# A hybrid decoder layer on one core: attention's value product, the embedding pairs and the norms' splits are moved

## The chip, the cores and the metric

One core of one Trainium2 chip runs the whole layer. The time is device microseconds (us) of one execution, as the median of three runs; a profiled execution of the same program gives the trace. The engines are TensorE (PE, with its weight loads as PEld), VectorE (DVE), ScalarE (ACT), GpSimd (POOL) and SyncE (SP), which issues most DMAs.

## The reference

One layer on 512 tokens of width 2048, in float32:

```python
h = rmsnorm(x, attn_norm_g)
u, v_sgu, q, k, v_att, g_a, g_b = split(h @ w_in)      # 2048 -> 9216
y_a = gelu(u) * (tril(w_s) @ rmsnorm(gelu(v_sgu)) + b_s)   # chunks of 128, 8 groups
z = q @ k.T * scale                                    # q, k normed; 8 heads of 128
log_1m = where(strict, log_sigmoid(-z), 0)
tail = reverse_cumsum(log_1m) - log_1m
w = where(strict, exp(log_sigmoid(z) + tail), 0)
y_b = w @ v_att
x = x + (sigmoid(g_a) * (y_a @ w_up_a) + sigmoid(g_b) * (y_b @ w_up_b)) @ w_o
gate, up = split(rmsnorm(x, ffn_norm_g) @ w_ffn_in)    # hidden 5632
x = x + (silu(gate) * up) @ w_ffn_out
x = x + sigmoid(rmsnorm(x, ple_norm_g) @ w_ple_gate) * (p @ w_ple)   # p: 256 wide
```

## The kernel before

Activations lie transposed: a block is 256 features by 512 tokens, kept as 128 partitions by 1024. Every float32 operand is split into a rounded high half and a low half (`split_into`, `Weights`): ACT writes the high half, DVE the difference, and three products make one. A **form** is a block of an operand in this shape. A *plain* use of a unit takes the four blocks of the form, twelve matmuls of 512 columns; a form of kind "S" has three further sums of blocks, and an "S" use takes seven products of half the size with them, on DVE's and ACT's account. `HALF` and the like say for each unit in how many of the first output blocks it is used plainly, since its sums are not there yet. A **pair** is one output block of 256 features: all units of the operand against its weights, accumulated in PSUM banks (six of tag "ps", two of tag "small"). A pair of "S" uses alone is *doubled*: two products stand side by side in a bank, and `mix_doubled` adds them up while the products go on; a pair with both kinds is put together by `rest`.

The order of work is written out in program order. Each unit of a pair calls `tick` once or twice; a tick loads or splits a part of the next forms (`builds`), loads the further sums' raw block (`seconds`, `fetch_second`), and runs what is due in `waiting`. `after(n, f)` runs f n ticks later. `Staged` and `beside` spread a chain of steps over ticks. Weights come through `planned` and `prepared` in a fixed order.

The stages: one embedding product (`ple_pair`: four blocks of `w_ple` against p, twelve matmuls of 512), then the projection `w_in` in four rounds of q, k, v and gate pairs, with the attention of two heads of the round before running beside them; SGU pairs; then the **merge**, plain pairs of `w_up_b` and `w_up_a` (eight of each); the **output projection** `w_o`, eight pairs, which adds onto x, stores x1 and sums its squares (`Norm.add`); the FFN's 44 pairs of `w_ffn_in` (the forms `fs` made from x1); three passes of `w_ffn_out`; and the eight gate pairs (forms `gs` from x2). Embedding products 3 to 7 stand at the end of the output projection. A norm's row is not needed for its products: it scales their outputs. `Norm.steps` sums with ones on PE, takes a power on POOL, and spreads the result with four small matmuls.

In attention a head has four blocks of keys j = 3, 2, 1, 0, each of (4 - j) x 128 queries. `stage_a` makes the logits, `stage_m` masks, `stage_b` and `stage_c` split the sums (L1122 on ACT, L1126 on DVE, into `zh` and `zl`), `stage_d` multiplies with a triangle (L1132, L1133), subtracts (L1137) and takes the exponential (L1138); `finish` multiplies a head's weights with the values (L1145) and copies the result (L1147). One block takes three ticks. Lines used below: L357 and L354, high and low half of weights; L373, weight sums; L284, L285, halves of forms; L520, the scaling by a norm's gain; L525, sums of blocks of forms; L683, products of S uses; L294 to L296, of plain ones; L739 and L742, mixing; L787, `rest`; L792, the addition onto x; L873, eviction of an embedding product; L516, loads.

## Time and profile before

| | |
|---|---|
| runs (us) | 2669.71, 2667.64, 2671.62; median 2669.71 |
| profiled execution (us) | 2668.2; span 2666.5, granted clock 0.998 |
| PE busy | 2640.4 us, 99% of the span |
| DVE, ACT, POOL busy | 84%, 53%, 17% |
| DMA | 560.16 MB, mean 210 GB/s |

Lnnn is a line of the kernel. In a list of waits a row reads: who waited, for whom, us in total, times, the longest. In a timeline: start, duration, engine, line, operation, names, and in brackets the idle time before it and what ended it. In a table by windows: the stretch, its length, busy us (instructions) of PE, PEld, DVE, ACT and POOL, the granted clock, the DMA share and GB/s. A row of groups ends with busy us, mean ns of one, and the engine's idle time before them.

### The profile page before, as it was taken

The numbers are of one execution on the slowest core, as the hardware profiler recorded it, in microseconds if no ns is written. First come the engines' busy times: TensorE is split into PE (matmuls) and PEld (weight loads), VectorE is DVE, ScalarE is ACT, GpSimd is POOL, SyncE is SP. The second block draws the span as 40 slices with busy tenths as digits, with TensorE's granted clock in tenths as the row PEclk, the third lists the DMA queues.
The fourth block names the chain that finished last, engine by engine and source line by source line (L and its number), as shares of the span: only waits on it lengthen the run. The fifth ranks groups of instructions, "written<-read, shape, count | busy, mean of one in ns | idle before, by whom it ended". The sixth has DMA issues, their size and how long they took to land.

```text
span 2666.5 us, 42598 instructions
## 1 busy us (share of the span) xinstructions
PE 2640.4 (99%) x15354; PEld 2312.4 (87%) x15354; DVE 2236.4 (84%) x3791; ACT 1413.9 (53%) x2245; POOL 453.4 (17%) x557
## 2 busy tenths in 40 slices
PE   8999999999999999999999999999999999999999
PEld 7888898888998888888888888888888888889898
DVE  8687878787887658989889888888889989989876
ACT  7656565655554334576444444444445445455643
POOL 0222322222220001101111111111110211211010
PEclk9999999999999999999999999999999999999999
DMA  7577777677775669988888878888787989988884
GB/s 227 158 190 174 185 173 187 171 182 197 179 188 186 214 212 264 239 265 223 220 218 207 210 194 207 203 203 202 197 209 223 263 220 277 226 248 246 252 229 134
DMA packets 293875, 560.16 MB, mean 210 GB/s; under 512 B 26400, under 2 KB 140832, under 8 KB 293664
## 3 DMA queue, kind: packets, MB, share of 16 engines
q1 hardware_dynamic: 231408, 442.08, 50.4%
q0 software_dynamic: 62256, 115.37, 27.0%
q8 instruction: 120, 1.97, 0.3%
q14 instruction: 91, 0.75, 0.1%
HBM read 505.97 MB, written 51.38 MB: 209 GB/s over the span
## 4 chain that ended last, share of the span: by engine, by line
PE 88%; DVE 5%; ACT 2%; DMA 2%; issue 1%; POOL 0%; SPq 0%; POOLq 0%; DVEq 0%; ACTq 0%
PE ps L683 49%; PE ps L295 10%; PE ps L296 10%; PE ps L294 10%; PE small L683 6%; DVE wlo L354 2%; DVE out L742 1%; PE small L1145 1%; PE small L1021 1%; DMA wholes<-x 1%; DMA wholes<-w_in 1%; ACT whi L357 1%; DVE wholes L373 0%; PE small L1095 0%; DVE parts L285 0%
## 5 line engine op out<-in xcount | busy, mean ns | idle before, releaser
L683 PE MATMUL ps<-parts,whi 128*128 128x512 f32 x4200 | 1404.7, 398 | 3.7 <-DVE out L787 3.1
L357 ACT ACTIVATE whi<-wholes 128x512 fp32r<-128x512 f32 (+3 forms) x941 | 872.5, 940 | 727.6 <-DVE wholes L373 270.5
L354 DVE TENSOR_TENSOR wlo<-wholes,whi 128x512 fp32r<-128x512 f32 (+3 forms) x941 | 982.7, 1079 | 65.8 <-ACT whi L357 64.0
L683 PEld LDWEIGHTS ps<-parts,wlo 128*128 128x128 f32 x4200 | 788.9, 188 | 178.4 <-DVE wlo L354 1.1
L683 PE MATMUL ps<-parts,wlo 128*128 128x256 f32 x4200 | 832.0, 279 | 0.0
L683 PEld LDWEIGHTS ps<-parts,whi 128*128 128x128 f32 x4200 | 676.4, 189 | 10.2 <-issue 4.5
L294 PE MATMUL ps<-parts,whi 128*128 128x256 f32 (+1 forms) x1822 | 598.9, 330 | 8.0 <-ACT parts L284 5.6
L295 PE MATMUL ps<-parts,whi 128*128 128x256 f32 (+1 forms) x1838 | 605.9, 330 | 0.8 <-DVE parts L285 0.8
L296 PE MATMUL ps<-parts,wlo 128*128 128x256 f32 (+1 forms) x1838 | 605.8, 330 | 0.0
L295 PEld LDWEIGHTS ps<-parts,whi 128*128 128x128 f32 x1838 | 348.4, 190 | 39.0 <-DVE parts L285 2.4
L294 PEld LDWEIGHTS ps<-parts,whi 128*128 128x128 f32 x1822 | 344.6, 190 | 41.5 <-ACT parts L284 6.7
L296 PEld LDWEIGHTS ps<-parts,wlo 128*128 128x128 f32 x1838 | 348.8, 190 | 30.8
L373 DVE TENSOR_TENSOR wholes<-wholes 128x256 f32<-128x256 f32 x822 | 345.1, 420 | 21.7 <-DMA wholes<-w_ffn_in 2.6
L742 DVE TENSOR_TENSOR out<-out,ps 128x256 f32<-128x256 f32 x490 | 202.9, 416 | 149.9 <-ACT out L739 149.4
L361 POOL DMA_DIRECT2D wholes<-w_ffn_in x170 | 148.0, 870 | 691.2 <-DVE wholes L373 197.4
L361 POOL DMA_DIRECT2D wholes<-w_in x132 | 116.3, 882 | 523.1 <-DMA wholes<-w_in 146.8
L683 PE MATMUL small<-parts,whi 128*128 128x512 f32 x480 | 190.3, 396 | 0.0
L285 DVE TENSOR_TENSOR parts<-wholes,parts 128x1024 fp32r<-128x1024 f32 (+3 forms) x148 | 138.1, 945 | 23.0 <-ACT parts L284 23.0
L284 ACT ACTIVATE parts<-wholes 128x1024 fp32r<-128x1024 f32 (+3 forms) x148 | 119.3, 830 | 55.1 <-DVE wholes L525 33.3
L739 ACT ACTIVATE out<-ps 128x256 f32<-128x256 f32 x258 | 95.7, 382 | 49.9 <-PE ps L683 46.4
L361 POOL DMA_DIRECT2D wholes<-w_ffn_out x64 | 55.6, 869 | 358.3 <-DMA wholes<-w_ffn_out 136.5
L1395 ACT ACTIVATE out<-out 128x512 f32<-128x512 f32 x44 | 27.9, 634 | 159.2 <-DVE out L1394 159.2
(123 smaller groups left out, 1750.2 us busy)
## 6 DMA issues: line engine op xcount, KB each, us to landing
wholes<-w_ffn_in SPq DMA_DIRECT2D x170, 384.0 KB, 5.6
wholes<-w_in SPq DMA_DIRECT2D x132, 384.0 KB, 5.0
wholes<-w_ffn_in SPq DMA_DIRECT2D x170, 256.0 KB, 4.8
wholes<-w_ffn_in POOLq DMA_DIRECT2D x170, 256.0 KB, 5.4
wholes<-w_in SPq DMA_DIRECT2D x132, 256.0 KB, 4.0
wholes<-w_in POOLq DMA_DIRECT2D x132, 256.0 KB, 5.0
wholes<-w_ffn_out SPq DMA_DIRECT2D x64, 384.0 KB, 6.3
wholes<-x SPq DMA_DIRECT2D x45, 512.0 KB, 5.6
```

The source lines that it names most:

```text
L284: return (nc.scalar.activation(hi, src, AF.Copy), nc.vector.tensor_tensor(out=lo, in0=src, in1=hi.bitcast(F32), op=ALU.subtract))
L285: nc.vector.tensor_tensor(out=lo, in0=src, in1=hi.bitcast(F32), op=ALU.subtract))
L294: nc.tensor.matmul(ps, sh, mh, start=start, stop=False)
L295: nc.tensor.matmul(ps, sh, ml, start=False, stop=False)
L296: return nc.tensor.matmul(ps, sl, mh, start=False, stop=stop)
L354: in_turn(nc.vector.tensor_tensor(out=self.lo[:, blocks], in0=r, in1=h.bitcast(F32), op=ALU.subtract))
L357: in_turn(nc.scalar.activation(h, r, AF.Copy))
L361: nc.gpsimd.dma_start(out=raw[:, 3:5], in_=self.src[:, 1:3], accum_op=ALU.add)
L373: in_turn(nc.vector.tensor_tensor(out=o, in0=x, in1=y, op=ALU.add))
L683: m = nc.tensor.matmul(out, l, r, start=first and k == 0, stop=last and k == 1)
L739: in_turn(nc.scalar.activation(out, x, AF.Copy, scale=scale))
L742: in_turn(nc.vector.tensor_tensor(out=out, in0=x, in1=y, op=op))
```

## The change

- Attention: `finish(0)` moves from the middle of the first block of head 1 to the start of its second, two ticks later; the last block of the round gets one tick more between `stage_c` and `stage_d`. So that head 1 does not overwrite what head 0 still needs, the weights of the third key block have two places (`w2`), and only 128 of a row are kept in `first`; the row additions in `stage_d` are cut to match.
- `tick`: a second load may go out in a tick that also runs a step, and is held back by every form of its stage that is not loaded yet, not only by the first three.
- The embedding products 3 to 7 stand behind five of the merge's pairs; their operand is made after the first.
- Forms with a gain are split with it: ACT scales while it writes the high half, DVE's fused operation writes the low half, and the scaling pass before goes.
- `FFN_UNTIL` replaces `HALF` for the FFN: units 2 and 3 are plain in its second pair too.
- The first hidden block and the first gate block take their norm's row three ticks after their pair; the gate's rows e and x2 are loaded three ticks into a pair; the norm keeps its accumulator for the row.

The diff:

```diff
@@ -38,2 +38,4 @@
 PLACE = 7 * 256
+LATER = 3
+FFN_UNTIL = 1, 1, 2, 2, 2, 2, 2, 2
 
@@ -220,6 +222,6 @@
             builds.popleft().step()
-        elif seconds and fits([(wholes, 5 * 256, "old")]):
+        if seconds:
             f = (urgent or seconds)[0]
-            if f.used or not any(b.stage == f.stage and b.ready() and not b.there
-                                 for b in list(builds)[:AHEAD]):
+            if (f.used or not any(b.stage == f.stage and b.ready() and not b.there
+                                  for b in builds)) and fits([(wholes, 5 * 256, "old")]):
                 f.fetch_second()
@@ -533,3 +535,12 @@
         x = form.operand()
-        split_into(x[:, 0:4, 0], x[:, 0:4, 1], cut(raw.f()))
+        if gain:
+            gi, k = gain
+            for i in range(2):
+                hi, lo = (x[:, 2 * i : 2 * i + 2, s] for s in range(2))
+                r, g = cut(raw.f(i * T, (i + 1) * T)), gcol[:, gi + 2 * k + i : gi + 2 * k + i + 1]
+                nc.scalar.activation(hi, r, AF.Copy, scale=g)
+                nc.vector.scalar_tensor_tensor(out=lo, in0=r, scalar=g, in1=hi.bitcast(F32),
+                                               op0=ALU.mult, op1=ALU.subtract)
+        else:
+            split_into(x[:, 0:4, 0], x[:, 0:4, 1], cut(raw.f()))
         give(raw)
@@ -594,4 +605,2 @@
             w = form.raw()
-            if gain:
-                gained(w.f(), w.f(), *gain)
             yield
@@ -959,3 +968,2 @@
                                  start=True, stop=True)
-            give(self.acc)
             yield
@@ -970,3 +978,3 @@
             yield
-            self.block = take(T)
+            self.block = self.acc
             nc.scalar.activation(self.block.f(), ps, AF.Copy)
@@ -1004,4 +1012,4 @@
 
-        for tag, n in (("l", T), ("w0", T), ("w1", 3 * P), ("w2", 2 * P), ("w3", 2 * P),
-                       ("first", 5 * P), ("k", 1024), ("v", 1024), ("zs", 1024)):
+        for tag, n in (("l", T), ("w0", T), ("w1", 3 * P), ("w2", 4 * P), ("w3", 2 * P),
+                       ("first", 2 * P), ("k", 1024), ("v", 1024), ("zs", 1024)):
             att[tag] = take(n)
@@ -1083,3 +1091,3 @@
         def weights(h, j):
-            return a_tile(f"w{j}", (NT - j) * P, (j == NT - 1) * h * P)
+            return a_tile(f"w{j}", (NT - j) * P, (j >= NT - 2) * h * (NT - j) * P)
 
@@ -1087,3 +1095,3 @@
 
-            return (sums(j) if j == NT - 1 else a_tile("first", (NT - j) * P, (j == 1) * 2 * P))[0:1]
+            return (sums(j) if j == NT - 1 else a_tile("first", P, (j == 1) * P))[0:1]
 
@@ -1114,3 +1122,3 @@
                 if j:
-                    nc.gpsimd.tensor_copy(first(j), s[0:1])
+                    nc.gpsimd.tensor_copy(first(j), s[0:1, :P])
                 nc.gpsimd.memset(s[0:1, :P], 0.0)
@@ -1134,4 +1142,6 @@
             if j:
-                nc.vector.tensor_tensor(out=sums(j - 1)[0:1, P:], in0=tp[0:1], in1=first(j),
-                                        op=ALU.add)
+                row = sums(j - 1)[0:1]
+                tt(row[:, P : 2 * P], tp[0:1, :P], first(j), ALU.add)
+                if n > P:
+                    tt(row[:, 2 * P :], tp[0:1, P:], sums(j)[0:1, P:], ALU.add)
             nc.vector.tensor_tensor(out=w, in0=w, in1=tp, op=ALU.subtract)
@@ -1160,6 +1170,6 @@
             ahead = blocks[i + 1 : i + 3]
+            if i == NT + 1:
+                finish(0)
             stage_b(j)
             yield 1
-            if i == NT:
-                finish(0)
             stage_c(j)
@@ -1168,2 +1178,4 @@
             yield 1
+            if not ahead:
+                yield 1
             stage_d(h, j)
@@ -1265,8 +1277,8 @@
                 plan((w_up_a if b == "a" else w_up_b)[j], "PPPP")
+            if 0 < j < 6:
+                planned.append((w_ple[j + 2].rearrange("p (b c) -> p b c", b=4), 1, "P"))
         for j in range(KU):
             plan(w_o[j], now("S" * KU, HALF, j))
-        for j in range(3, KU):
-            planned.append((w_ple[j].rearrange("p (b c) -> p b c", b=4), 1, "P"))
         for m in range(KH):
-            plan(w_ffn_in[m], now("S" * KU, HALF, m))
+            plan(w_ffn_in[m], now("S" * KU, FFN_UNTIL, m))
         at = 0
@@ -1356,2 +1368,8 @@
                 after(1, lambda j=j, s=s: store("mix", j, s))
+        if not j:
+            ple_operands()
+        elif j < 6:
+            ple_pair(j + 2)
+            if j == 5:
+                ple_done()
     give(norm1.block)
@@ -1361,8 +1379,4 @@
     fs = [spilled_form("S", "x1", j, (g_ffn, j)) for j in range(KU)]
-    raw = deque([load(xT[0])])
     for j in range(KU):
-        if j < KU - 1:
-            raw.append(load(xT[j + 1]))
-        if j == KU - 1:
-            after(3, ple_operands)
+        h = load(xT[j])
         if j == 1:
@@ -1370,6 +1384,2 @@
         pr = pair(ms, last=j == KU - 1, j=j, until=HALF, doubled=7)
-        if j == KU - 1:
-            ple_pair(3)
-            ple_pair(4)
-        h = raw.popleft()
         pr.onto(h.f())
@@ -1379,5 +1389,2 @@
         give(h)
-    for j in range(5, 8):
-        ple_pair(j)
-    ple_done()
 
@@ -1392,3 +1399,3 @@
     def hidden(m, o):
-        g = o[:, :T]
+        g, row2 = o[:, :T], norm2.row()
         nc.vector.tensor_tensor(out=g, in0=g, in1=row2, op=ALU.mult)
@@ -1404,7 +1411,8 @@
             build(hs[0])
-        o = pair(fs, last=m == KH - 1, j=m, until=HALF, doubled=7).out()
-        if m == 0:
-            row2 = norm2.row()
+        o = pair(fs, last=m == KH - 1, j=m, until=FFN_UNTIL, doubled=7).out()
         st = Staged(hidden(m, o))
-        st.step()
+        if m:
+            st.step()
+        else:
+            after(LATER, st.step)
         if m == KH - 1:
@@ -1427,3 +1435,3 @@
             o = pr.out()
-            scaled(o, row2)
+            scaled(o, norm2.row())
             if not end:
@@ -1440,6 +1448,9 @@
     for j in range(KU):
-        e, x2 = load(ple_spill[j]), load(spill["x2", j])
+        rows = []
+
+        def rest(j=j, rows=rows):
+            rows.extend((load(ple_spill[j]), load(spill["x2", j])))
 
-        def finish(o, a, b, ps=None):
-            s = o[:, a:b]
+        def finish(o, a, b, ps=None, j=j, rows=rows):
+            s, row3 = o[:, a:b], norm3.row()
             if ps is not None:
@@ -1456,6 +1467,12 @@
             nc.scalar.activation(s, s, AF.Sigmoid)
-            nc.vector.tensor_tensor(out=s, in0=s, in1=e.f(a, b), op=ALU.mult)
-            nc.vector.tensor_tensor(out=s, in0=s, in1=x2.f(a, b), op=ALU.add)
+            for r, op in zip(rows, (ALU.mult, ALU.add)):
+                nc.vector.tensor_tensor(out=s, in0=s, in1=r.f(a, b), op=op)
             nc.sync.dma_start(out=outT[j][:, a:b], in_=s)
 
+        def close(o, finish=finish, rows=rows):
+            finish(o, 0, 2 * T)
+            give(*rows)
+
+        if j:
+            after(LATER, rest)
         if j == KU - 1:
@@ -1464,5 +1481,7 @@
             o = pair(gs, j=j, until=GATE_UNTIL).out()
-            row3 = norm3.row()
-            finish(o, 0, 2 * T)
-            give(e, x2)
+            if j:
+                close(o)
+            else:
+                rest()
+                after(LATER, lambda close=close, o=o: close(o))
     finish_waiting()
```

ACT in round 1 of attention, around the exponential of head 0's last block (L1138, the row with 128x512) and the copy of the product with the values (L1147); L739 belongs to a projection's mixing. Before:

```order
L357 ACTIVATE whi_80<-wholes 128x1280
L1138 ACTIVATE wholes<-wholes 128x512
L739 ACTIVATE out_2867<-ps_2691 128x256
L739 ACTIVATE out_2867<-ps_2696 128x256
L1147 ACTIVATE wholes<-small_2849 128x512
L739 ACTIVATE out_2867<-ps_2701 128x256
```

After, where the two are L1148 and L1157, and L1105 to L1108 are a later block's `stage_a`:

```order
L1108 ACTIVATE wholes<-wholes 128x256
L1148 ACTIVATE wholes<-wholes 128x512
L1130 ACTIVATE parts<-wholes 128x128
L748 ACTIVATE out_2867<-ps_2696 128x256
...
L1106 ACTIVATE wholes<-small_2907,rr_2189 128x384
L1148 ACTIVATE wholes<-wholes 128x128
L1130 ACTIVATE parts<-wholes 128x256
L1157 ACTIVATE wholes<-small_2933 128x512
L359 ACTIVATE whi_78<-wholes 128x512
```

The copy stands three rows below the exponential before, fourteen below it after, behind the first exponential of head 1 (128x128).

SP at the end of the output projection, where the last block of x1 (x_782, then x_786) is stored and loaded again; L875 stores an embedding product, the other loads of x are first or second loads of forms. Before:

```order
L875 DMA ple_10810<-out_10793 128x1024
L1376 DMA x_782_8254<-wholes 128x1024
L339 DMA wholes<-w_ffn_in 128x2x256
L341 DMA wholes<-w_ffn_in 128x768
L875 DMA ple_10843<-out_10826 128x1024
L875 DMA ple_10875<-out_10858 128x1024
L516 DMA wholes<-x_782_8254 128x1024
L339 DMA wholes<-w_ffn_in 128x2x256
L341 DMA wholes<-w_ffn_in 128x768
L875 DMA ple_10908<-out_10891 128x1024
L516 DMA wholes<-x_775_8247 128x1024
```

After:

```order
L339 DMA wholes<-w_ffn_in 128x1024 x2
L518 DMA wholes<-x_782_8266 128x1024
L1386 DMA x_786_8270<-wholes 128x1024
L518 DMA wholes<-x_779_8263 128x1024
L339 DMA wholes<-w_ffn_in 128x1024
L518 DMA wholes<-x_786_8270 128x1024
L518 DMA wholes<-x_780_8264 128x1024
L341 DMA wholes<-w_ffn_in 128x2x256
L343 DMA wholes<-w_ffn_in 128x768
L518 DMA wholes<-x_781_8265 128x1024
```

The embedding stores are gone from there, and a second load (x_779) now stands between the store and the load of the last block.

DVE at the end of the output projection's second pair, where `rest` (L787, then L796) frees two banks; L285 and L287 are low halves of forms, L354 and L356 of weights. Before:

```order
L525 TENSOR_TENSOR wholes<-wholes 128x256
L285 TENSOR_TENSOR parts<-wholes,parts 128x256
L354 TENSOR_TENSOR wlo_77<-wholes,whi_76 128x1280
L354 TENSOR_TENSOR wlo_77<-wholes,whi_76 128x512
L285 TENSOR_TENSOR parts<-wholes,parts 128x3x256
L787 TENSOR_TENSOR out_9527<-ps_9512,out_9527 128x512
L787 TENSOR_TENSOR out_9527<-ps_9505,out_9527 128x512
L373 TENSOR_TENSOR wholes<-wholes 128x256
L792 TENSOR_TENSOR wholes<-wholes,out_9527 128x1024
```

After:

```order
L287 TENSOR_TENSOR parts<-wholes,parts 128x3x256
L375 TENSOR_TENSOR wholes<-wholes 128x256
L287 TENSOR_TENSOR parts<-wholes,parts 128x256
L375 TENSOR_TENSOR wholes<-wholes 128x256
L287 TENSOR_TENSOR parts<-wholes,parts 128x256
L796 TENSOR_TENSOR out_9665<-ps_9648,out_9665 128x512
L356 TENSOR_TENSOR wlo_79<-wholes,whi_78 128x1280
L356 TENSOR_TENSOR wlo_79<-wholes,whi_78 128x512
L796 TENSOR_TENSOR out_9665<-ps_9641,out_9665 128x512
L375 TENSOR_TENSOR wholes<-wholes 128x256
```

The two releases stood side by side behind a weight split and a form's split; now the first stands behind the smaller splits, and a weight split stands between the two.

## The prediction

> **What bounds the kernel now.** I read the page first, then TensorE's waits, then the timeline around each wait that the change can reach, and last the DMA landings where the embedding pairs stood.
>
> ```profile
> span 2666.5 us, 42598 instructions
> PE 2640.4 (99%) x15354; PEld 2312.4 (87%) x15354; DVE 2236.4 (84%) x3791; ACT 1413.9 (53%) x2245; POOL 453.4 (17%) x557
> PE ps L294 <- ACT parts L284: 5.6, 3, 5.1
> PE ps L683 <- DVE out L787: 3.1, 1, 3.1
> PE small L1145 <- ACT wholes L1138: 2.5, 3, 0.8
> PE small L1133 <- DVE parts L1126: 1.6, 4, 0.7
> PE small L1145 <- issue: 0.8, 1, 0.8
> PE ps L294 <- ACT out L873: 0.6, 1, 0.6
> PE ps L295 <- DVE parts L285: 0.8, 2, 0.5
> ```
>
> The page puts TensorE (PE) at 2640.4 of 2666.5 us, so it is the bound, and the change removes none of its work. All that can be won is wait, and the remaining rows (us in total, times, longest) name the waits: 5.1 us of the first is the start of the program. The share of 99% flatters a little, because a record of PE ends after the next one has started:
>
> ```profile
> 1173.75 0.39 PE L296 MATMUL ps<-parts,wlo 128*128 128x512 f32 x1
> 1173.97 0.39 PE L294 MATMUL ps<-parts,whi 128*128 128x512 f32 x1
> 1175.42 0.50 PE L294 MATMUL ps<-parts,whi 128*128 128x512 f32 x1 [0.61 <-ACT out L873]
> 1199.74 0.28 PE L294 MATMUL ps<-parts,whi 128*128 128x256 f32 x1
> 1199.86 0.28 PE L295 MATMUL ps<-parts,whi 128*128 128x256 f32 x1
> ```
>
> Matmuls of 512 columns start about 0.227 us apart (1173.97 minus 1173.75, read over longer stretches) and last 0.39; those of 256 columns start 0.12 apart. So 0.16 us of each wait is hidden in the record before it, and I add 0.16 to every wait of the list. An embedding pair, twelve matmuls of 512, is 2.7 us of PE, and a plain unit of a projection the same.
>
> **Attention's first product with the values (L1145).** In round 1, PE and ScalarE (ACT):
>
> ```profile
> 287.51 0.62 PE L683 MATMUL ps<-parts,whi 128*128 128x512 f32 x2
> 288.98 1.10 PE L1145 MATMUL small<-wholes 128*128 128x512 f32 x2 [0.84 <-ACT wholes L1138]
> 287.06 1.26 ACT L357 ACTIVATE whi<-wholes 128x1280 fp32r<-128x1280 f32 x1
> 288.22 0.61 ACT L1138 ACTIVATE wholes<-wholes 128x512 f32<-128x512 f32 x1
> ```
>
> PE stands until ACT has written the last weights of head 0 (L1138, done at 288.83), which queued behind a weight split of 1.26 us. The four rounds are the 2.5 us in three waits and the 0.8 listed as "issue": 3.3 + 4 x 0.16 = 4.0 us. Two ticks later means two thirds of a block's 42 matmuls, about 28 x (0.227 + 0.12) / 2 = 4.9 us, against 1.0 us of wait: all **4.0 us** go. What is late next is the small PSUM bank that the product takes, released by VectorE (DVE) after stage_d of the next block; the order leaves 23 matmuls, 4 us, for that. The new copies of the weights (w2 doubled) cost nothing and remove DVE's wait on PE to reuse them. Between losing all and winning nothing I take all, since the exponential is done 3.9 us ahead.
>
> **Attention's last block (L1133).** The four waits on the low half of the sums:
>
> ```profile
> 317.95 0.39 PE L683 MATMUL ps<-parts,whi 128*128 128x512 f32 x1
> 318.75 0.50 PE L1133 MATMUL small<-parts,tri 128*128 128x512 f32 x1 [0.41 <-DVE parts L1126]
> 318.01 0.68 DVE L1126 TENSOR_TENSOR parts<-wholes,parts 128x512 fp32r<-128x512 f32 x1
> ```
>
> They are 1.6 + 4 x 0.16 = 2.2 us, 0.57 us each here. In the order the product moves back by five matmuls only (54 after the stage before, 49 then), 5 x 0.17 = 0.9 us, which still covers the mean wait and about the longest (0.7 + 0.16). I take **2.0 us**, with 0 and 2.2 as ends. The row additions that replace one 1x384 addition by two shorter ones are DVE's, one per block, and lie beside PE work.
>
> **The second loads come sooner.** The largest single wait stands in the output projection, where the first doubled pair needs banks that DVE's L787 must free:
>
> ```profile
> 1043.65 0.63 PE L683 MATMUL ps<-parts,whi 128*128 128x512 f32 x2
> 1047.37 0.47 PE L683 MATMUL ps<-parts,whi 128*128 128x512 f32 x1 [3.09 <-DVE out L787]
> 1043.60:1047.40 3.80, 0.71 (x5) 0.31 (x4) 3.80 (x6) 1.31 (x3) 0.89 (x1) 1.00 0.92 335
> 1049.00:1052.00 3.00, 3.00 (x12) 2.60 (x11) 2.69 (x5) 2.70 (x3) 0.88 (x1) 0.50 1.03 292
> DVE wholes L525 <- DMA wholes<-mix: 3.6, 2, 1.9
> L354 DVE TENSOR_TENSOR wlo<-wholes,whi 128x1280 fp32r<-128x1280 f32 x405 | 603.4, 1490 | 29.7 <-ACT whi L357 29.4
> L354 DVE TENSOR_TENSOR wlo<-wholes,whi 128x512 fp32r<-128x512 f32 x443 | 305.0, 689 | 18.7 <-ACT whi L357 18.4
> ```
>
> PE waits 3.09 + 0.16 = 3.3 us while DVE is busy for 3.80 of 3.80 us: L787 stands in a backlog of splits. Then the granted clock is 0.50 for 3.0 us, which costs 1.5 more. The wait is worth 4.8 us. Just before it, DVE had stood 3.6 us for the second loads of mix. The change lets such a load go out in a tick that also splits, and the order issues them one or two weight loads earlier on SP. If those 3.6 us go, L787 (L796 now) runs before its bank is needed. Against it, a weight split of 1.49 + 0.69 us now stands between the two bank releases. Ends: -4.8, and +2.2 if that split is what PE then waits for. I take **-3.5**: most of the wait, and the clock stays up.
>
> On the clock, the Trainium skill ("TensorE: Matmul & The Clock Gate", Part 1) says that PE falls to half rate after an idle window of about 3.4 us and needs as long to recover. The 0.50 behind the 3.3 us agrees; by that rule every shorter wait goes without the 1.5 us, so a half removed wait would still save it.
>
> **Embedding pairs moved.** Five pairs, 5 x 2.7 = 13.6 us of PE, leave the end of the output projection for the merge stage. Their PE time is the same there, and that stage has room (DVE 76.35, ACT 44.14 and DMA 0.64 of 130 us):
>
> ```profile
> 870.00:1000.00 130.00, 130.00 (x575) 107.67 (x574) 76.35 (x82) 44.14 (x43) 0.88 (x1) 1.00 0.64 215
> 1176.00:1200.00 24.00, 24.00 (x116) 19.99 (x116) 17.08 (x27) 18.32 (x26) 4.59 (x4) 1.00 0.96 328
> 1161.05 0.39 PE L294 MATMUL ps<-parts,whi 128*128 128x512 f32 x1
> 1164.35 0.42 DVE L742 TENSOR_TENSOR out<-out,small 128x256 f32<-128x256 f32 x1
> 1169.42 1.22 DVE L792 TENSOR_TENSOR wholes<-wholes,out 128x1024 f32<-128x1024 f32 x1
> x<-wholes SPq DMA_DIRECT2D x1, 512.0 KB, 5.1
> DMA to landing us min/median/max: 5.2/7.4/12.1
> L613 DVE SCALAR_TENSOR_TENSOR parts<-wholes,gcol,parts 128x512 fp32r<-128x512 f32 x6 | 4.4, 746 | 1.2 <-ACT parts L520 1.2
> L520 ACT ACTIVATE wholes<-wholes,gcol 128x512 f32<-128x512 f32 x68 | 45.7, 714 | 16.4 <-DMA wholes<-x 13.9 <-DMA wholes<-xT 1.4 <-DMA gcol<-gains 1.0
> L284 ACT ACTIVATE parts<-wholes 128x1024 fp32r<-128x1024 f32 x72 | 74.5, 1051 | 30.4 <-DVE wholes L525 10.7 <-DMA wholes<-y 10.0 <-DMA wholes<-mix 8.3
> ```
>
> But they were a cover. The projection ends where L294 begins, at 1161.05; the last block of x must then be mixed, added, stored, loaded again and split before the FFN's eighth unit. Mixing ends 3.7 us after 1161.05 (L742). In the new order a weight split of 1024 (some 1.2 us, as the addition) and two fused splits (2 x 0.75) stand before the addition (1.2): stored at 7.6. Storing lands after 5.1, the load after 5.2 at best and 7.4 in the median, ACT's first half takes 0.7: 18.6 to 20.8 us. Needed is it after seven units, 7 x 2.7 = 19.0, and some 1 us of the norm's small matmuls, 20. So PE waits 0 to 1 us there; with the 12.1 landing it would be 5.5. The second loads of forms 0 and 1, needed at the second pair, are as tight; today's waits on L284 and L285 in that place are 0.4 + 0.3 by the gaps, near 1.0 with the hidden part. I set 1.0 + 2.0 = 3.0 for the new entry, and today's bill is 0.77 (the 0.61 on L873) + 1.0 = 1.8: **+1.2 us**, with -1.8 and +5 as ends.
>
> **Smaller edits.** Two units of the FFN's second pair become plain: 24 more matmuls of 512 and 42 fewer of 256, 24 x 0.227 - 42 x 0.118 = **+0.5 us**, so that only two forms need second loads there. The fused gain takes two scalings of 0.714 and a split of 1.051 to two scalings on ACT, 13 times 1.05 us saved, and DVE pays 2 x 0.746 instead of 1.22, 13 x 0.27 more; both lie beside PE. The norm rows awaited three ticks later sit under plain products, 8 us of cover; without it DVE would stand for one load, at most the 7.4 above, before weight splits that run a unit ahead. The gate's norm keeps its place in the order: nothing.
>
> **Sum.** -4.0 - 2.0 - 3.5 + 1.2 + 0.5 = -7.8 us. The profiled execution took 2668.2 us, the runs 2667.64 to 2671.62 with median 2669.71; a difference of waits applies to either, and I set it against the median: **2661.9 us**. 0.2%, about what a measurement of this kernel can tell from no change, is 5.3 us.
>
> **Rivals.**
> - *DVE gets no further ahead* in the output projection: the order still has the same count of splits ahead of L796, and PE waits as today. -7.8 + 3.5: 2665.4. For it: DVE's 3.80 of 3.80. Against: the 3.6 us of DMA waits. 0.17.
> - *The first product's wait only changes its releaser* (the small bank, behind DVE's backlog, which in this stage delayed L1126 four times): -7.8 + 4.0, 2665.9. 0.10.
> - *Slower: the FFN's entry is bound by its loads.* In 1176 to 1200 the DMA engines were at 0.96, and the x loads took up to 12.1 us. The 13.6 us of cover are gone; if the queue, not the chain, sets the forms, all of that comes back as wait, and the half clock with 1.5. Without the +1.2 the other terms are -9.0, so it decides from about 9 us of wait on; whole, 2669.7 - 9.0 + 15.1 = 2675.8. Against: two of the four second loads that were due at the second pair are now due at the third. 0.08.
> - *Everything hides*: the loads land at their best, the entry costs nothing (-1.8), the whole 4.8 and 2.2 go: -4.0 - 2.2 - 4.8 - 1.8 + 0.5 = -12.3, 2657.4. 0.15. [...]
>
> **How the numbers follow.** The forecast keeps 0.50, with its own range of 2658.5 to 2665. The range of 2655.5 to 2670 takes in the two rivals above it and the one below, with 1 us on either side for the medians' scatter and up to 4 for a long landing; it leaves out the slow case. Below 2664.4 lie most of the forecast (0.43), the last rival (0.15) and some of the first two (0.07): faster 0.65, within 0.2% 0.25, slower 0.10.
>
> **What would show it.** Right: no wait of PE on L1138's successor, none over 0.3 us on the last block's low half, no clock of 0.50 after the projection's third pair, under 3 us of waits between the projection's end and the FFN's third pair. Wrong: a wait of the product on DVE; PE standing 3 us for L796 again; a load of x landing after its unit is due, with a half clock behind it.

## The result, and the profile after

The changed kernel took 2658.84 us (median of 5 runs, 2658.44 to 2659.74), the kernel before 2668.58 beside it (2665.47 to 2671.62): ratio 0.9957, 95% interval 0.9946 to 0.9968, 9.7 us less. The profiled execution took 2659.74, 8.5 less than that of before. Busy time by engine from its page, and all the waits of TensorE in its trace (total, times, longest, in us):

```profile
span 2658.0 us, 42554 instructions
PE 2638.2 (99%) x15336; PEld 2312.3 (87%) x15336; DVE 2234.6 (84%) x3821; ACT 1403.2 (53%) x2233; POOL 448.1 (17%) x556
PE ps L296 <- ACT parts L286: 5.3, 2, 5.1
PE small L1214 <- ACT wholes L1052: 2.2, 1, 2.2
PE ps L296 <- ACT whi L359: 2.1, 2, 1.9
PE small L1103 <- ACT wholes L1052: 1.0, 3, 0.4
PE ps L692 <- DVE out L796: 1.0, 2, 0.8
PE ps L692 <- DVE wlo L356: 0.9, 1, 0.9
PE ps L297 <- DVE parts L287: 0.5, 1, 0.5
PE ps L298 <- DVE wlo L356: 0.5, 1, 0.5
PE ps L692 <- ACT whi L359: 0.4, 1, 0.4
PE ps L692 <- DVE out L751: 0.2, 1, 0.2
```

No row is left of the first product with the values (L1155 now) or of the last block (L1141), and the wait of 3.1 us on L787 (L796 now) has become two of 1.0 together. New are the rows of L692 and L298 on weight splits (L356, L359), and the wait of L1214, the product of the gated unit at the end of the attention stage, has grown. In the kernel before it was:

```profile
PE small L1202 <- ACT wholes L1044: 1.0, 1, 1.0
```

To compare kernels whose stages lie a few us apart I add up, from the records of TensorE, by how much each matmul starts later than the usual pitch after the one before it (0.227 us behind 512 columns, 0.115 behind 256), from 0.06 us on. That counts the waits and also the slow matmuls at half clock. Sums in us by stage, one profiled execution each; the last column is the profiled time. That is one execution of several: in after, e2, e3, e6 and e8 it was the slowest of them, in e12 the fastest, so the medians below come first where they differ.

| kernel | attention 130-600 | gated unit 600-700 | merge 700-1000 | projection 1000-1150 | FFN entry 1150-1300 | 1950 to end | all | time |
|---|---|---|---|---|---|---|---|---|
| before | 28.6 | 1.9 | 2.1 | 4.9 | 2.5 | 3.5 | 53.4 | 2668.2 |
| after | 22.5 | 4.8 | 2.2 | 1.5 | 1.0 | 4.8 | 45.3 | 2659.7 |
| after, again (e5) | 22.6 | 1.7 | 2.0 | 2.4 | 1.0 | 5.3 | 44.3 | 2658.9 |
| e1 | 22.3 | 4.9 | 2.6 | 12.6 | 2.3 | 3.1 | 56.8 | 2670.8 |
| e9 | 22.5 | 4.3 | 1.7 | 7.7 | 4.2 | 6.5 | 55.1 | 2669.1 |
| e6 | 22.6 | 5.1 | 2.4 | 8.0 | 1.1 | 12.0 | 59.8 | 2674.9 |
| e2 | 22.3 | 4.9 | 3.9 | 2.8 | 1.0 | 3.1 | 47.2 | 2661.8 |
| e4 | 22.6 | 5.0 | 2.3 | 0.3 | 4.3 | 7.2 | 51.6 | 2666.3 |
| e3 | 22.7 | 4.8 | 2.3 | 2.3 | 5.6 | 4.5 | 51.1 | 2665.0 |
| e7 | 22.7 | 5.0 | 1.8 | 2.5 | 2.9 | 6.3 | 49.5 | 2663.9 |
| e8 | 22.5 | 3.8 | 4.8 | 1.8 | 1.1 | 7.7 | 50.0 | 2665.1 |
| e10 | 28.6 | 2.1 | 2.0 | 3.7 | 5.3 | 2.4 | 52.1 | 2667.8 |
| e11 | 22.5 | 2.6 | 2.2 | 2.6 | 1.4 | 3.7 | 43.7 | 2658.8 |
| e12 | 22.4 | 1.1 | 1.5 | 0.0 | 2.2 | 4.8 | 41.7 | 2656.3 |

(The start of the program and the first passes of the FFN, 8.0 to 9.7 and at most 0.5 us, are in "all" only.) The columns of before and after say where the time came from: attention 6.1 us, the output projection 3.4, the FFN's entry 1.5 and the start of the program 1.2, together 12.2; 2.9 us went back at the gated unit and 1.3 in the last quarter. What is left is the 8 us of the "all" column. Two of these are not shown to be the change's: the start differs by some 0.6 between the two profiles of the changed kernel, and the gated unit by 3.1.

**Attention.** Round 1, the first product and the last weights it needs (PE, ACT):

```profile
290.74 2.39 PE L1155 MATMUL small<-wholes 128*128 128x512 f32 x8
283.89 0.62 ACT L1148 ACTIVATE wholes<-wholes 128x512 f32<-128x512 f32 x1
```

The weights of head 0 are ready at 284.51, the product starts at 290.74 with no idle time in front of it.

**The output projection.** A window, PE's and DVE's timeline at the first doubled pair, and DVE's wait for mix:

```profile
1050.00:1055.00 5.00, 4.03 (x22) 3.02 (x21) 5.00 (x8) 1.57 (x4) 0.89 (x1) 1.00 0.90 259
1050.48 0.50 PE L692 MATMUL ps<-parts,whi 128*128 128x512 f32 x1 [0.17 <-DVE out L796]
1053.17 0.47 PE L692 MATMUL ps<-parts,whi 128*128 128x512 f32 x1 [0.80 <-DVE out L796]
1050.34 1.48 DVE L356 TENSOR_TENSOR wlo<-wholes,whi 128x1280 fp32r<-128x1280 f32 x1
DVE wholes L527 <- DMA wholes<-mix: 1.2, 1, 1.2
```

DVE is as busy as before (5.00 of 5.00), but ahead of this it stood 1.2 us for the second loads of mix instead of 3.6. The first release costs PE 0.3 us; then the weight split (L356) that the order put between the two releases makes it wait for the second, 1.0. The clock stays at 1.00.

**The FFN's entry.** The first matmul (PE), the last row of x added and split (DVE, ACT, DVE), and its unit (PE):

```profile
1165.98 0.39 PE L296 MATMUL ps<-parts,whi 128*128 128x512 f32 x1
1171.46 1.22 DVE L801 TENSOR_TENSOR wholes<-wholes,out 128x1024 f32<-128x1024 f32 x1
1184.20 1.32 ACT L541 ACTIVATE parts<-wholes,gcol 128x512 fp32r<-128x512 f32 x2
1184.94 1.41 DVE L542 SCALAR_TENSOR_TENSOR parts<-wholes,gcol,parts 128x512 fp32r<-128x512 f32 x2 [0.44 <-ACT parts L541]
1186.47 0.40 PE L296 MATMUL ps<-parts,whi 128*128 128x512 f32 x1
```

The addition ends 6.7 us behind the FFN's first matmul, the split's first half 19.7 and its second 20.4. Counted by matmuls the eighth unit begins at 1186.47, 20.5 behind, without a wait. The margin is tenths of a us, and e10 below lacks it.

### The profile page after: what moved, and what is told of

Read it like the earlier page. It is cut to its first block, busy times and chain, and to the rows that moved or that the text cites. A ratio compares the mean times of both kernels' runs of the same rounds, so it can differ in the third digit from the quotient of the medians.

```text
span 2658.0 us, 42554 instructions
## 1 busy us (share of the span) xinstructions
PE 2638.2 (99%) x15336; PEld 2312.3 (87%) x15336; DVE 2234.6 (84%) x3821; ACT 1403.2 (53%) x2233; POOL 448.1 (17%) x556
## 4 chain that ended last, share of the span: by engine, by line
PE 90%; DVE 4%; DMA 3%; issue 1%; ACT 1%; SPq 0%; POOL 0%; ACTq 0%; POOLq 0%; DVEq 0%
PE ps L692 53%; PE ps L298 10%; PE ps L297 9%; PE ps L296 9%; PE small L692 6%; DVE wlo L356 1%; DVE wholes L527 1%; DMA wholes<-w_ffn_out 1%; PE small L1103 1%; PE small L1155 1%; DVE parts L287 1%; PE small L1029 1%; DMA x<-wholes 1%; ACT whi L359 0%; PE small L1214 0%
## 5 line engine op out<-in xcount | busy, mean ns | idle before, releaser
L692 PE MATMUL ps<-parts,whi 128*128 128x512 f32 x4200 | 1409.4, 398 | 1.6 <-DVE out L796 1.0
L359 ACT ACTIVATE whi<-wholes 128x512 fp32r<-128x512 f32 (+2 forms) x940 | 871.5, 941 | 745.8 <-DVE wholes L375 286.6
L356 DVE TENSOR_TENSOR wlo<-wholes,whi 128x512 fp32r<-128x512 f32 (+2 forms) x940 | 979.4, 1076 | 73.7 <-ACT whi L359 73.0
L692 PEld LDWEIGHTS ps<-parts,wlo 128*128 128x128 f32 x4200 | 790.2, 188 | 178.2 <-issue 1.9
L692 PE MATMUL ps<-parts,wlo 128*128 128x256 f32 x4200 | 831.3, 279 | 0.9 <-DVE wlo L356 0.9
L692 PEld LDWEIGHTS ps<-parts,whi 128*128 128x128 f32 x4200 | 677.1, 189 | 10.5 <-issue 3.6
L298 PE MATMUL ps<-parts,wlo 128*128 128x256 f32 (+1 forms) x1832 | 604.9, 331 | 0.5 <-DVE wlo L356 0.5
L298 PEld LDWEIGHTS ps<-parts,wlo 128*128 128x128 f32 x1832 | 347.3, 190 | 32.4 <-DVE wlo L356 1.6
L375 DVE TENSOR_TENSOR wholes<-wholes 128x256 f32<-128x256 f32 (+1 forms) x820 | 345.0, 421 | 17.9 <-DVE wlo L356 1.4
L751 DVE TENSOR_TENSOR out<-out,ps 128x256 f32<-128x256 f32 x490 | 202.3, 416 | 147.6 <-ACT out L748 147.4
L692 PE MATMUL small<-parts,whi 128*128 128x512 f32 x480 | 190.3, 397 | 0.0
L287 DVE TENSOR_TENSOR parts<-wholes,parts 128x1024 fp32r<-128x1024 f32 (+3 forms) x137 | 122.8, 907 | 18.5 <-ACT parts L286 18.5
L286 ACT ACTIVATE parts<-wholes 128x1024 fp32r<-128x1024 f32 (+3 forms) x137 | 106.5, 800 | 54.2 <-DVE wholes L527 35.7
```

The costliest lines, as they stand in the source:

```text
L286: return (nc.scalar.activation(hi, src, AF.Copy), nc.vector.tensor_tensor(out=lo, in0=src, in1=hi.bitcast(F32), op=ALU.subtract))
L287: nc.vector.tensor_tensor(out=lo, in0=src, in1=hi.bitcast(F32), op=ALU.subtract))
L298: return nc.tensor.matmul(ps, sl, mh, start=False, stop=stop)
L356: in_turn(nc.vector.tensor_tensor(out=self.lo[:, blocks], in0=r, in1=h.bitcast(F32), op=ALU.subtract))
L359: in_turn(nc.scalar.activation(h, r, AF.Copy))
L375: in_turn(nc.vector.tensor_tensor(out=o, in0=x, in1=y, op=ALU.add))
```

## The experiments

Each is compared with the kernel before on its own chip (medians there 2671.31 for e1 to e4, 2672.28 for e5 to e8, 2670.65 for e9 to e12); 0.001 in a ratio is 2.7 us, and the intervals reach about that far to either side, so differences of 2 or 3 us between two runs are read from the profiles and not clear of the times' noise. My theory was the prediction's: every part is worth the wait that it removes. The rival, which the runs came to favour, is that the parts cover for each other at two bottlenecks, the start of the doubled pairs in the projection and the FFN's entry.

**e5, the changed kernel again.**

> The changed kernel unchanged, beside the others on this chip, to see which of its waits come again. Theory: the waits at 640 (2.4 us) and on L796 in the output projection (0.3 and 1.0) come from the order and come again; the ones of 2200 to 2420 us (2.8 us together) depend on when a load lands and will be elsewhere or gone. Time 0.9957 of before, within 0.15%. Rival: the late waits are of the order too and stand in the same places.

Ratio 0.9955 (0.9942 to 0.9967), median 2658.89. Which waits come again (PE's waits, of the whole run and of 2190 to 2450 us):

```profile
PE ps L692 <- DVE out L796: 2.0, 3, 1.1
PE small L1214 <- ACT wholes L1052: 0.8, 1, 0.8
PE ps L692 <- DVE wlo L356: 0.9, 1, 0.9
PE ps L692 <- ACT whi L359: 0.4, 1, 0.4
```

The waits on L796 came again; the other two I had the wrong way round. The late pair of 0.9 and 0.4 stands in the same place (2242 to 2244 us): it is of the order. L1214's wait is 0.8 here and 2.2 there. Half of the difference is that GpSimd issues a load, with the power that the product needs right behind it, at 637.17 us here and at 637.93 there; the other half is that PE comes to the place 0.7 us later here.

**e1, attention alone; e10, all but attention.**

```
             # e1: before with these hunks; e10: the changed kernel without them
+            if i == NT + 1:
+                finish(0)
             stage_b(j)
             yield 1
-            if i == NT:
-                finish(0)
...
+            if not ahead:
+                yield 1
             stage_d(h, j)
```

> The kernel before with the attention part of the change alone (first product two ticks later, last block one tick, weights' copies doubled, row addition in two pieces). Theory, the prediction's first two terms: the four waits on L1138 (1.0 us each) and the four on L1126 (0.37 to 0.82) go and nothing takes their place: 6.3 us less than before, 2662.3. Rival: the wait of 1.2 us at the end of the stage (L1202 on L1044, 2.4 in the changed kernel) grows because of this part: 5.1 less, 2663.5. Second rival: the product then waits on its bank behind VectorE: 2 us less, 2666.6.

> The changed kernel with attention as before. Theory: the waits of the first product (4 x 1.0) and of the last block (2.3 in all) come back, the wait of the gated unit's product falls from 2.4 to about 1.2: 5 us above the changed kernel, 0.9975 of before. Rival: as the part added to the kernel before gave only 0.9989, it is worth 3 us or less here too: 0.9967.

e1: 0.9989 (0.9979 to 0.9999), median 2667.57 against 2671.31. e10: 0.9985 (0.9976 to 0.9993), median 2667.48, slower than both the theory and the rival had it; kernels with the part beside it took 2661.24 (e11) and 2660.39 (e12). The column of the stage says 28.6 without and 22.3 to 22.7 with the part, in all twelve other profiles alike: 6.1 us, the prediction's 6.0. But e1 pays 3.0 of them at the gated unit, and in its profile more at the projection:

```profile
PE ps L683 <- DVE out L787: 4.0, 1, 4.0
PE small L1206 <- ACT wholes L1044: 2.4, 1, 2.4
```

e10's rows hold the old waits (2.5 and 0.7 for the first product, 1.7 for the last block), and its column has 4.3 us more at the FFN's entry, which nothing in the edit touches:

```profile
PE small L1153 <- ACT wholes L1146: 2.5, 3, 0.8
PE small L1141 <- DVE parts L1134: 1.7, 3, 0.9
PE small L1153 <- issue: 0.7, 1, 0.7
```

At the FFN's entry, DVE's and PE's timeline:

```profile
1191.29 1.41 DVE L542 SCALAR_TENSOR_TENSOR parts<-wholes,gcol,parts 128x512 fp32r<-128x512 f32 x2 [2.69 <-ACT parts L541]
1193.05 0.68 PE L941 MATMUL small<-diag,ones 128*128 128x128 f32 x4 [1.75 <-DVE diag L939]
```

Of these 4.3 us, 1.9 are the chain of the last row of x. Its split ends at 1192.70, 20.6 us behind the FFN's first matmul (1172.09), as late as in the changed kernel; here all of the norm's small operands (L939) stand behind it in DVE's queue, and PE waits for the first of them. Another 2.1 are two waits for weight splits at 1228 and 1230.

So the part's 6 us in its stage are shown; what it is worth to the end (about 3 from before, about 7 from after, with intervals of 2 to 3 us on either side) depends on what the later stages do with another start.

**e4, the old rule for second loads; e2, the pairs back at the projection's end; e6, both; e9, attention and the new rule alone.**

```
+        elif seconds and fits([(wholes, 5 * 256, "old")]):       # e4, e6; e9 has the new rule
-        if seconds:
             f = (urgent or seconds)[0]
...
+        if j == KU - 1:                                          # e2, e6, and their plan
+            ple_pair(3)
+            ple_pair(4)
...
-        elif j < 6:
-            ple_pair(j + 2)
```

> The changed kernel with the old rule for second loads (only in a tick that builds nothing, and looking only three builds ahead). Theory, the prediction's third term: the wait of 3.3 us on L796 and 1.5 us of half clock come back in place of today's 0.3 and 1.0, 3.5 us more; but the new waits of the last third (2243 to 2245, 2280 and 2419 us, 2.5 us together) are the price of the same rule and go: about 2659.8. Rival: those late waits have another cause: 2662.3. Second rival: the wait on L796 does not come back, because the moved embedding pairs removed it: 2656 to 2659.

> The changed kernel with the five embedding pairs back at the end of the output projection. Theory: the pairs' place is worth only what stood around them, the 0.77 us on L873, since at the entry of the FFN the last row of x comes just in time without their cover: 2659.6, and no wait over 1 us on L796. Rival: the earlier pairs are what took the queue and VectorE's load off the projection, and the 3.3 us wait with its half clock comes back: 2663. Second rival: the cover was worth something, and with it the time falls below 2658.

> The changed kernel with both the old rule for second loads and the embedding pairs at the projection's end. Either alone left no 3 us wait on L796. Theory: each of the two was enough to remove it, so with both undone it stands there again, 3.3 us or more with a half clock behind it, and with it 1 to 3 us at the projection's entry: 4 to 6 us above the changed kernel, 0.9975 of before. Rival: a third edit (the rows of x no longer loaded one tick ahead, the fused split) removed it, and it stays away: 1 to 2 us above the changed kernel.

> The kernel before with the attention part and the new rule for second loads, everything else (pairs, fused split, awaited rows, units of the FFN) as before. Theory: the rule alone is enough to remove the wait on L787 with its half clock (4.2 us and more with the attention part alone), so it gains 4 to 6 us on the kernel with the attention part alone: about 0.997 of before, and no wait over 1.3 us on L787. Rival: in the changed kernel it was the fused split or the later load of x that made the room, and the wait stays: 0.9985 to 1.0.

e4 0.9973 (0.9964 to 0.9982), e2 0.9948 (0.9935 to 0.9962), e6 0.9999 (0.9990 to 1.0008), e9 0.9997 (0.9988 to 1.0007). PE's largest row of waits between 1000 and 1060 us in e2, e6 and e9 (in e4 the view lists none), and what DVE stood there for mix in e6:

```profile
PE ps L297 <- DVE parts L287: 1.5, 2, 0.8
```

```profile
PE ps L692 <- DVE out L796: 4.8, 1, 4.8
DVE wholes L527 <- DMA wholes<-mix: 3.8, 2, 3.2
```

```profile
PE ps L683 <- DVE out L787: 6.1, 1, 6.1
```

In the changed kernel either of the two is enough against the long wait on L796: undoing one leaves 0.3 (e4) or 2.8 us (e2, none of it on L796) in the projection, undoing both brings back a wait of 4.8 and 8.0 us. e2's theory held, and e4's did not: my second rival for e4 was right for this place, the late waits stayed, and e4 is some 4 us slower than the changed kernel, with 4.3 us at the FFN's entry and 7.2 in the last quarter. e6 with all other edits is no faster than before, 12 us above the changed kernel, twice what I expected. Some 7 of the 12 lie in the last quarter, where the largest row waits for forms; why both edits together bring them is open:

```profile
PE ps L296 <- ACT parts L286: 3.9, 2, 2.7
```

e9's expectation failed: put into the kernel before, the rule does not remove the wait (6.1). So the rule works only with something else of the change, the fused split, the row of x loaded a pair later (one block of memory less is held) or another; which, is open, as the pairs alone on the kernel before are. What the moved pairs do is seen in the store of mix (KB, median us to landing; before, then after):

```profile
mix<-wholes SPq DMA_DIRECT2D x8, 512.0 KB, 6.5
```

```profile
mix<-wholes SPq DMA_DIRECT2D x8, 512.0 KB, 3.6
```

With 13.6 us of matmuls put between the weights of the merge stage, its stores land in 3.0 to 3.7 us in all kernels with five pairs there, and in 6.5 to 6.9 in those with none. DVE's waits for mix in 1000 to 1055 us follow: 0 to 2.3 us with the pairs there, 3.0 to 4.6 without. At the FFN's entry the same two seem to cover for each other: 4.3 us in e4 (old rule, no pairs there), 1.0 in e2, 1.1 in e6 and 1.0 in after. That does not hold for every order, since e10 has the new rule as after has it and pays 5.3 there. e4's wait, in PE's timeline:

```profile
1193.03 0.39 PE L296 MATMUL ps<-parts,whi 128*128 128x256 f32 x1 [1.69 <-ACT parts L286]
```

On the other side the two late waits, 1.6 us with their hidden parts near 2243, stand in after, e4, e5, e7, e8 and e11, and not in e2; that makes up for most of e2's extra in the projection and the merge, and it is as fast as the changed kernel (ratio 0.9948). But e3, e10 and e12, with pairs in the merge stage, don't have them either: what decides is not the pairs' place alone, and no run isolates more.

**e3, four doubled units from the FFN's second pair on.**

```
-FFN_UNTIL = 1, 1, 2, 2, 2, 2, 2, 2
+FFN_UNTIL = 1, 1, 1, 1, 2, 2, 2, 2
```

> The changed kernel with four doubled units instead of two from the FFN's second pair on (FFN_UNTIL equal to HALF). Theory: 0.5 us of matmuls saved, but the second loads of forms 2 and 3, which land at 1188.5 and 1195.1 us in the changed kernel, are then due at about 1193 instead of a pair later, with 2.5 us of VectorE and ScalarE work behind each landing: PE waits 3 to 5 us at the second pair, with a half clock if it is one wait: 2662 to 2665. Rival: the loads go out earlier when they are asked for earlier, and only 0.5 us changes: 2658.3.

0.9968 (0.9956 to 0.9981), median 2662.35, some 3 us above the changed kernel, with overlapping intervals. The theory held in part, in smaller pieces and with no half clock: PE's waits from 1140 to 1260 us, where the changed kernel has none.

```profile
PE ps L296 <- ACT parts L286: 0.9, 2, 0.8
PE ps L692 <- DVE wlo L356: 0.9, 1, 0.9
PE ps L692 <- ACT whi L359: 0.8, 1, 0.8
PE ps L297 <- DVE parts L287: 0.4, 1, 0.4
```

The waits for forms (L286, L287), about 2 us with their hidden parts, are what the theory named. The two for weights (L356, L359), again about 2, stand at 1223 and 1225; e10, with the FFN's units as in the changed kernel, has them as well.

**e7, the gain apart from the split; e11, the norms' rows not awaited.**

```
             w = form.raw()
+            if gain:                                             # e7
+                gained(w.f(), w.f(), *gain)
...
-            after(LATER, st.step)                                # e11, and the last stage's rows
+            st.step()
```

> The changed kernel with the norm's gain applied in a step of its own before the split, as before. Theory: at the FFN's entry the last row of x was ready for PE with nothing to spare (its split ended at 1186.35, PE used it from 1185.8 to 1186.7); two scalings of 0.71, a split of 1.05 on ScalarE and one of 1.22 on VectorE in place of 0.71 and two of 0.75 make it 1.1 to 1.5 us later, and PE waits that long; the gate's entry likewise, about 1.1 (the wait on L932 of before). 1.5 to 2.5 us above the changed kernel. Rival, the prediction's term: both forms lie beside PE's work, 0.

> The changed kernel with the norms' rows not awaited three ticks later (the FFN's first gate and the last stage's rows at once, as before). Theory, the prediction's 0: under plain products nothing of it ends a wait of PE, within 1 us of the changed kernel, 0.9955 of before. Rival: VectorE then stands for the row of the norm (the last of its chain is ready about 3 us after the first unit) ahead of splits that PE needs, and PE waits 1 to 3 us at the second pair of the FFN or of the gate: 0.996 to 0.9967.

e7: 0.9967 (0.9957 to 0.9978), median 2663.46 against e5's 2658.89, more than the 1.5 to 2.5 us that I expected. The place is another too: the waits of 1140 to 1260 us stand at the end of the projection, where the mixing (L744, which is L751 in the changed kernel) waits in DVE's queue behind the forms' splits, not at the last row of x.

```profile
PE ps L296 <- DVE out L744: 0.9, 1, 0.9
PE ps L685 <- DVE out L744: 0.4, 1, 0.4
```

With its hidden part the first is 1.1 of the 1.9 us that the FFN's entry has over that of after; the second, 0.5, stands at 1150, just ahead of that column. Ahead of the two splits there DVE stands 2.0 and 1.9 us for ACT, which scales and splits the whole block first. The other 2 to 3 us lie in columns that vary between executions. e11: 0.9958 (0.9945 to 0.9970): nothing, as predicted.

**e8, the gated unit's product a tick later; e12, three pairs in the merge stage and two behind the projection.**

```
             times(gv, ps, rr)
-            yield 2
+            yield 3                                              # e8
...
-        elif j < 6:
+        elif j < 4:                                              # e12; pairs 6 and 7 behind w_o
             ple_pair(j + 2)
```

> The changed kernel with the product of the gated unit (L1214) one tick later, which puts 16 matmuls of the projection, 3.0 us, ahead of it. Theory: the 2.4 us that PE stands at 640 us, for the power on GpSimd and the scaling behind it, are covered: 2.4 us less than the changed kernel, 0.9948 of before. Rival: the chain waits on something that comes later as well (the queue on GpSimd), and the wait stays or moves to the next norm of the unit: 0 to 1 us less.

> The changed kernel with three of the embedding pairs in the merge stage and two behind the output projection, after its last row of x. Theory: with the new rule neither place needs the whole cover; 8.2 us of pairs bring the last mix block in time at the projection's entry and 5.4 us stand over the entry of the FFN: no wait over 1 us at either place, and the 1.6 us at 2243 us may go as they do with all pairs at the end: 2657, 0.995 of before. Rival: half a cover is none, and both places wait 1 to 2.5 us: 0.9965.

e8: 0.9966 (0.9954 to 0.9978), median 2663.36, some 3 to 4.5 us slower than the changed kernel. The wait at 640 went, but the later norms of the unit, which had none, got two (1.2 and 1.6 us at 726 and 770), and two products behind transposes another 0.9 each:

```profile
PE small L1214 <- ACT wholes L1052: 2.5, 2, 1.4
PE ps L692 <- DVE wholes L751: 0.7, 1, 0.7
PE ps L692 <- DVE out L751: 0.7, 1, 0.7
```

e12: 0.9957 (0.9944 to 0.9969), median 2660.39, the same as the changed kernel. The projection has nothing left (0.0), the entry 2.2 instead of 1.0, and other waits of 1.2 and 0.4 stand at 2094, one of 1.0 at 2386. Its theory held at the first place and not quite at the second. No version tried is clearly faster than the changed kernel.

## Why the prediction was right

The time was 2658.8 against 2661.9, inside the forecast's own range, 0.3 us from its lower end; the difference of medians in the same runs is 9.7 us against 7.8. The signs that the prediction had named for being right all came in this order, and none of those for being wrong. Its steps, one by one:

- **First product and last block, -4.0 and -2.0**: 6.1 us, and 5.9 to 6.3 in each kernel that has the part. The rival of a wait that only changes its releaser is out: no row of L1155 remains.
- **Second loads, -3.5**: -3.4 in one profile and -2.5 in the other, with the split between the two bank releases as the rest, as the text had named it. But the credit, given to the rule alone, does not hold. On top of the other edits either is enough, the pairs without the rule (e4) or the rule without the pairs (e2), and the rule in the kernel before is not (e9). The DMA waits of 3.6 us did shrink, with the 13.6 us of matmuls in the merge stage, which the prediction priced at nothing. In e2, though, the wait on L796 went while DVE stood 3.0 us for mix, so that row is not the whole cause; how the rule does it is open. Nor is the place safe: e10, with both, has a wait of 1.9 us on L796 and a half clock behind it.
- **The FFN's entry, +1.2**: came out at -1.5, the one term with the wrong sign. The new entry cost 1.0 us where 3.0 were set, the old one 2.5 where 1.8 were counted. The chain of the last row of x was worked out at 18.6 to 20.8 us against 20 needed; it took 20.4 against 20.5, so that step held, by tenths of a us: in e10 it took 20.6 and cost PE 1.9. The 2.0 us set for the second loads of forms 0 and 1 did not come. Two edits that the prediction counted in other places bear on them: the units taken out of the second pair (about 2 us of waits for forms in e3) and the new rule (3.3 in e4's column).
- **Smaller edits, +0.5 and 0**: PE runs 18 matmuls fewer, 24 more of 512 columns and 42 fewer of 256, as counted. Their +0.5 is not to be seen: the time outside the sums is 0.4 and 0.2 us less than before in the two profiles. The awaited rows are worth nothing (e11). The fused split is not: "both lie beside PE" failed in e7, because DVE's queue, not its time, is what the mixing at the projection's end stands in.
- **Not in the prediction**: the gated unit's chain, which an earlier end of attention leaves uncovered (2.9 us in one profile, none in the other), and 1.3 to 1.8 us more in the last quarter, most of it the waits at 2243. Together up to 4.2 us, they about cancel the 2.7 us by which the entry came out better and the start's 1.2, neither of them foreseen. So it is luck that the total is nearer than its terms.

On the half clock the traces spoke against the sentence from the Trainium skill ("TensorE: Matmul & The Clock Gate", Part 1), which the prediction had drawn on for its 3.4 us: a wait of 1.82 us was followed by a clock of 0.51, as the last section shows.

## What to carry to other kernels

Where two edits each hide the same late chain, pricing them one at a time gives the credit to the wrong one and can double or lose it: undo each, and then both, before saying what a part is worth. A wait that is removed early in a pipelined kernel comes back in part wherever a chain on another engine had used it as cover; look for the next product whose operands have a fixed latency. And in a kernel with full queues ask of a new instruction not only whether its engine has time, but what is queued behind it.

## What the runs showed of the hardware

Waits well under 3 us can bring the half clock. Rows of PE, and the windows of 3 us behind them (the clock is the last figure but two), in after, e9, e5 and e4 in turn:

```profile
640.32 0.38 PE L1214 MATMUL small<-wholes 128*128 128x128 f32 x1 [2.23 <-ACT wholes L1052]
640.30:643.30 3.00, 2.98 (x13) 2.79 (x13) 0.75 (x1) 1.90 (x4) 0.92 (x1) 0.54 0.71 104
```

```profile
639.41 0.38 PE L1206 MATMUL small<-wholes 128*128 128x128 f32 x1 [1.82 <-ACT wholes L1044]
640.40:643.40 3.00, 3.00 (x12) 2.61 (x11) 1.17 (x2) 1.30 (x3) 0.92 (x1) 0.51 0.59 80
```

```profile
639.60:642.60 3.00, 3.00 (x20) 2.78 (x21) 1.17 (x2) 2.56 (x6) 0.92 (x1) 1.00 0.91 228
```

```profile
1193.00:1196.00 3.00, 2.97 (x24) 2.97 (x25) 2.36 (x2) 0.96 (x2) 0.86 (x1) 1.00 0.31 63
```

After listed waits of 2.23 and 1.82 us the clock is 0.54 and 0.51 for 3 us; after 0.75 (e5) and 1.69 (e4, the row shown above) it stays at 1.00. At the program's start a wait of 1.9 left it at 1.00 too. Over all fourteen profiles, behind their first 10 us, no listed wait under 1.78 us has a half clock behind it; of six between 1.78 and 1.93 four have it and two have not; all longer ones have it. So the line lies near 1.8 us here and is not sharp. Behind it a wait costs some 1.5 us more than it shows, which is about half of what separates the gated unit's 4.8 us in after from its 1.7 in e5.
